# Two 64-byte spacers in an encoder block: the transposed input and the last two 14 KB places move by 64 bytes in SBUF

## The chip, the cores and the metric

The kernel runs on one core of one Trainium2 chip. The metric is device time in microseconds (us) of one execution; lower is better. SBUF addresses below are bytes within a partition, the same in all 128 partitions.

## What is computed

One bidirectional encoder block on x of 512 x 2048, in float32:

```
h = rmsnorm(x); q, k, v of 16 heads = h @ w_in
heads 0-7:  three dilated windows, merged by their softmax denominators   (group A)
heads 8-15: softmax(q1 k1) - lambda * softmax(q2 k2), times v, rmsnorm    (group B)
x = x + concat(heads) @ w_out
h = rmsnorm(x)
x = x + (silu(h @ w_gate) * (h @ w_up)) @ w_down        # inner width 5632
out = rmsnorm(x)
```

## The kernel before, in words

Every large product is made of three matmuls in the float32r type (`mm3`, lines 183 to 186): each operand is split into a high part and the rest, and high x high, high x low and low x high are added up in PSUM. A matmul has a stationary operand, 128 columns loaded into TensorE by a weight load, and a moving operand of 256 or 512 columns streamed through it. The profile names a matmul by its operands, the moving one first: `bank<-xt,hi` streams `xt` against stationary `hi`.

The order on TensorE is the order of the code (a manual schedule); side work of attention (`attend_a`, `attend_b`) is mixed in step by step. The stages, in order of time:

- `unit_v` and `unit_qk` (lines 221 to 293): the values of two heads, then queries and keys of each head, from the transposed input `xt`: 16 tiles of 128 x 1024 (512 high, 512 low), 4 KB per partition each. In `unit_v` `xt` is stationary and the weights `hi`, `lo` move, 256 columns. In `unit_qk` the weights are stationary and `xt` moves, 512 columns; six matmuls follow each other, then a step of attention may stand between.
- `unit_out` (lines 452 to 495): the output projection. The 16 heads' outputs (`mix_tile`, line 500) are stationary: ten in 4 KB tiles `m0` to `m9`, the last six in `w0` and `w1`, two places of 14 KB (7 x 512 floats) that hold three each. The weights `hi`, `lo` move, 512 columns.
- `unit_gu` (lines 649 to 722): gate and up projections, 44 units of 7 products (Strassen-like). In a product 8 operands, `cp0` to `cp5` and then `w0` and `w1`, move against the weights (`hi`, `lo`, or `m6` to `m9`), 3 matmuls of 256 columns each: 24 in a product.
- `unit_first`, `unit_dn`, `unit_last` (lines 768 to 907): the down projection. In `unit_dn` the operands `cp` (and `w0` for pairs 7 and 14) are stationary, the weights move, 256 columns. In `unit_last` the stationary operand lies in a `cp` place; of the eight weight pairs that move, 512 columns, three lie in `hi` and `lo` and five in `cp` places (`last_pair`, line 878).

Where tiles lie. Pools are allocated from both ends of SBUF, left and right. All the large tiles are multiples of 512 bytes long, so every tile of a pool has the same address modulo 128, and so has every slice that a matmul takes. In the built program of the kernel before, the left side (`st`, `hi`, `lo`, then `xt`, and after the heads `m0` to `m9`, `w0`, `w1` in the place of `xt`) lies at 32 modulo 128. The right side (`at`, `cp`, `y`, `wk` and the rest) lies at 96. So of the matmuls of 256 and 512 columns some have both operands at the same place modulo 128, and some have them 64 bytes apart:

| matmuls | stage | columns | moving, stationary before | after |
|---|---|---|---|---|
| `hi,xt` `lo,xt` | unit_v | 256 | 32, 32 | 32, 96 |
| `xt,hi` `xt,lo` | unit_qk | 512 | 32, 32 | 96, 32 |
| `hi,w` `lo,w` | unit_out, 6 of 16 heads | 512 | 32, 32 | 32, 96 |
| `hi,m` `lo,m` | unit_out, the other 10 | 512 | 32, 32 | the same |
| `cp,hi` `cp,lo` `cp,m` | unit_gu, 6 of 8 operands | 256 | 96, 32 | the same |
| `w,hi` `w,lo` `w,m` | unit_gu, 2 of 8 operands | 256 | 32, 32 | 96, 32 |
| `hi,cp` `lo,cp` `m,cp` | unit_dn | 256 | 32, 96 | the same |
| `hi,w` `lo,w` `m,w` | unit_dn, pairs 7 and 14 | 256 | 32, 32 | 32, 96 |
| `hi,cp` `lo,cp` | unit_last, 3 of 8 pairs | 512 | 32, 96 | the same |
| `cp,cp` | unit_last, 5 of 8 pairs | 512 | 96, 96 | the same |

The column "after" is what the change below makes of it.

Of the kernel before, what the change touches and what calls it, by code (L numbers as in the profile page):

```python
# [10 lines left out]
F32 = mybir.dt.float32  # L11
# [6 lines left out]
P = 128  # L18
# [27 lines left out]
def encoder_block(ctx: ExitStack, tc: tile.TileContext, io):  # L46
    nc = tc.nc
    pe, act, dve, pool = nc.tensor, nc.scalar, nc.vector, nc.gpsimd
# [14 lines left out]
    def stage(name, bufs, side="left"):  # L63
        return tc.alloc_tile_pool(name=name, bufs=bufs, side=side, reuse_waits="tile")

    bigx = stage("bigx", KT)
    half = stage("half", 16, "right")
    early = stage("early", 1, "right")
    biga = stage("biga", KT, "right")
    pools = {}  # L70
# [206 lines left out]
    def unit_head(h):  # L277

        qk = unit_qk(h)
        if h % 2 == 0 and h < 2 * H - 2:  # L280
            values_of[0] = unit_v(h // 2 + 1)
        for i in range(KT):
            next(qk)
            yield
            if h < 2 * H - 2 and i % 8 == 7:
                for _ in range(4):
                    next(values_of[0])
                    yield
        for _ in qk:
            pass  # L290
        if h % 2 and h < 2 * H - 2:
            for _ in values_of[0]:
                pass
# [158 lines left out]
    def unit_out(c):  # L452
        xr = []
        b = [bank() for _ in range(NT)]
        for kb in range(8):
            wh, wl = batch()
            if c == 3 and kb == 4:
                load_unit(0)
            if c == 3 and kb == 7:
                for n in PRODUCTS[:2]:  # L460
                    make(0, n)
            if kb == 6:
                for t in range(NT):
                    piece = w_tile()
                    nc.sync.dma_start(piece, io["x"][t * P:(t + 1) * P, c * 512:(c + 1) * 512])
                    xr.append(piece)
            for k2 in range(2):
                k = kb * 2 + k2
                if c == 0:
                    while k not in done:  # L470
                        advance()
                    m = mix_tile(k)
                    act.copy(m[:, :512], mixes[k])
                    dve.tensor_sub(m[:, 512:], mixes[k], m[:, :512].bitcast(F32))
                    mixes[k] = m
                m = mixes[k]
                ws = slice(k2 * 512, (k2 + 1) * 512)
                for t in range(NT):
                    mm3(b[t], m[:, t * P:(t + 1) * P], m[:, 512 + t * P:512 + (t + 1) * P], wh[:, ws], wl[:, ws],
                        start=k == 0, stop=k == KT - 1)  # L480
                yield
# [15 lines left out]
    def place(i, dt=F32):  # L497
        return pools["mx"].tile([P, 1024], dt, name=f"m{i}")

    def mix_tile(k):  # L500

        if k < 10:
            return place(k, F32R)
        j, i = divmod(k - 10, 3)
        if i == 0:
            mix_tile.last = pools["mx"].tile([P, 7, 512], F32R, name=f"w{j}")
        return mix_tile.last[:, 2 * i:2 * i + 2].rearrange("p a q -> p (a q)")
# [442 lines left out]
    def drive(unit, rate=1):  # L950
        for _ in unit:
            for _ in range(rate):
                advance()
# [32 lines left out]
    for h in range(2 * H):  # L986
        drive(unit_head(h))
    bigx.release()
    pools["mx"] = stage("mx", 1)
    for c in range(4):  # L990
        drive(unit_out(c), 2 if c == 0 else 1)
# [62 lines left out]
def _build(arrays):  # L1054
    import concourse.bacc as bacc

    nc = bacc.Bacc("TRN2", target_bir_lowering=False, num_devices=1, dynamic_dma_scratch_size=1024)
    io = {n: nc.dram_tensor(n, a.shape, mybir.dt.from_np(a.dtype), kind="ExternalInput").ap()
          for n, a in arrays.items()}
    io["out"] = nc.dram_tensor("out", (S, D), F32, kind="ExternalOutput").ap()  # L1060
    with tile.TileContext(nc) as tc:
        encoder_block(tc, io)
    return nc
# [9 lines left out]
```

## Time and profile before

| what | us |
|---|---|
| median of 3 runs | 2227.66 (2226.16 to 2230.18) |
| the profiled execution, its own time | 2229.82 |
| its span, first to last instruction | 2228.0 |
| TensorE busy within the span | 2195.6 (99%) |
| VectorE, ScalarE busy | 1663.9, 999.4 |
| mean granted TensorE clock | 0.992 |

The profile is of one execution. A matmul's duration in it runs from its start to the modelled end of its pipeline, and matmuls overlap: what TensorE takes for one in a stream is the distance from its start to the start of the next (called pitch below), not its duration.

### The profile page before, as it was taken

How to read it: one execution, taken by the hardware profiler on the slowest of the kernel's cores; microseconds unless marked ns; L12 is line 12 of the kernel's file. 1: busy time of each engine (PE TensorE's matmuls, PEld its weight loads, DVE VectorE, ACT ScalarE, POOL GpSimd, SP SyncE). 2: the span in 40 equal slices, each digit the busy share in tenths (PEclk: the TensorE clock that was granted, in tenths of full speed). 3: DMA queues.
4: the chain of work that ended last, by engine and by line, in shares of the span. 5: the costliest groups of instructions: out<-in, count | busy, mean ns of one | idle time of the engine just before them, and what ended most of it. 6: DMA issues, size and time to landing. Idle time of an engine off the chain costs nothing.

```text
span 2228.0 us, 37887 instructions
## 1 busy us (share of the span) xinstructions
PE 2195.6 (99%) x15754; PEld 2067.2 (93%) x15754; DVE 1663.9 (75%) x2373; ACT 999.4 (45%) x1486; POOL 10.4 (0%) x23
## 2 busy tenths in 40 slices
PE   9999999999999999999999999999999999999997
PEld 8888888888888888999999999999999899999995
DVE  5655555676787447888888888888887597888897
ACT  6333333545555344454444544445444443343443
POOL 0000000000000000000000000000000000000000
PEclk9999999999999999999999999999999999999999
DMA  8222222222222552354454444544445736446344
GB/s 301 84 78 76 85 77 76 76 76 68 67 76 91 165 180 85 124 169 147 132 169 147 165 147 134 170 147 159 151 132 164 312 114 245 156 166 236 114 138 138
DMA packets 86908, 308.59 MB, mean 139 GB/s; under 512 B 10032, under 2 KB 11952, under 8 KB 84304
## 3 DMA queue, kind: packets, MB, share of 16 engines
q1 hardware_dynamic: 81696, 267.11, 36.4%
q0 software_dynamic: 2736, 34.87, 3.8%
q10 hardware_dynamic: 2304, 4.20, 0.5%
q8 instruction: 123, 2.02, 0.4%
q14 instruction: 49, 0.40, 0.1%
HBM read 261.31 MB, written 44.83 MB: 137 GB/s over the span
## 4 chain that ended last, share of the span: by engine, by line
PE 92%; DVE 4%; DMA 2%; ACT 1%; issue 1%; SPq 0%; ACTq 0%; DVEq 0%
PE bank L184 30%; PE bank L186 29%; PE bank L185 29%; PE bank L303 1%; DMA acts_kept<-raw 1%; DVE lo L630 1%; PE bank L403 1%; PE bank L404 1%; DMA st<-w 0%; DVE m L630 0%; PE bank L539 0%; PE bank L428 0%; DMA combos<-y 0%; DMA at<-xT 0%; ACT hi L629 0%
## 5 line engine op out<-in xcount | busy, mean ns | idle before, releaser
L629 ACT CAST hi<-m 128x1024 fp32r<-128x1024 f32 (+1 forms) x208 | 215.0, 1038 | 252.9 <-PE bank L185 125.0
L184 PE MATMUL bank<-cp,hi 128*128 128x256 f32 x1116 | 314.1, 281 | 0.0
L185 PE MATMUL bank<-cp,hi 128*128 128x256 f32 x1116 | 312.2, 280 | 0.0
L186 PE MATMUL bank<-cp,lo 128*128 128x256 f32 x1116 | 312.2, 280 | 0.0
L630 DVE TENSOR_TENSOR lo<-m,hi 128x1024 fp32r<-128x1024 f32 (+1 forms) x208 | 249.6, 1201 | 61.8 <-ACT hi L629 61.5
L121 DVE TENSOR_TENSOR lo<-st,hi 128x1024 fp32r<-128x1024 f32 (+1 forms) x136 | 165.1, 1214 | 141.0 <-ACT hi L120 140.2
L120 ACT CAST hi<-st 128x1024 fp32r<-128x1024 f32 (+1 forms) x136 | 141.7, 1042 | 192.8 <-PE bank L185 74.8
L185 PE MATMUL bank<-lo,cp 128*128 128x256 f32 (+1 forms) x738 | 211.4, 286 | 4.2 <-DVE lo L630 2.7
L184 PE MATMUL bank<-hi,cp 128*128 128x256 f32 (+1 forms) x738 | 211.3, 286 | 0.3 <-ACT hi L120 0.3
L184 PEld LDWEIGHTS bank<-cp,hi 128*128 128x128 f32 x1116 | 211.1, 189 | 0.3 <-DVE wk L679 0.2
L186 PE MATMUL bank<-hi,cp 128*128 128x256 f32 (+1 forms) x738 | 211.0, 286 | 0.0
L185 PEld LDWEIGHTS bank<-cp,hi 128*128 128x128 f32 x1116 | 210.6, 189 | 0.0
L186 PEld LDWEIGHTS bank<-cp,lo 128*128 128x128 f32 x1116 | 210.5, 189 | 0.0
L184 PE MATMUL bank<-xt,hi 128*128 128x512 f32 x512 | 206.3, 403 | 0.0
L184 PE MATMUL bank<-cp,m 128*128 128x256 f32 x732 | 205.6, 281 | 0.1
L186 PE MATMUL bank<-cp,m 128*128 128x256 f32 x732 | 204.2, 279 | 0.0
L185 PE MATMUL bank<-cp,m 128*128 128x256 f32 x732 | 204.2, 279 | 0.0
L186 PE MATMUL bank<-xt,lo 128*128 128x512 f32 x512 | 200.4, 391 | 0.0
L185 PE MATMUL bank<-xt,hi 128*128 128x512 f32 x512 | 199.9, 391 | 0.0
L629 ACT CAST m<-m 128x1024 fp32r<-128x1024 f32 (+1 forms) x112 | 116.8, 1043 | 148.6 <-PE bank L185 88.6
L630 DVE TENSOR_TENSOR m<-m,m 128x1024 fp32r<-128x1024 f32 (+1 forms) x112 | 135.3, 1208 | 41.4 <-ACT m L629 41.2
L185 PE MATMUL bank<-lo,xt 128*128 128x256 f32 x512 | 145.1, 283 | 0.6 <-DVE lo L121 0.6
(276 smaller groups left out, 5920.7 us busy)
## 6 DMA issues: line engine op xcount, KB each, us to landing
st<-w SPq DMA_DIRECT2D x199, 512.0 KB, 3.7
m<-w SPq DMA_DIRECT2D x180, 512.0 KB, 4.4
cp<-combos POOLq DMA_DIRECT2D x17, 1792.0 KB, 16.6
combos<-y SPq DMA_DIRECT2D x57, 512.0 KB, 4.4
combos<-y SPq DMA_DIRECT2D x19, 256.0 KB, 5.2
m<-w SPq DMA_DIRECT2D x12, 384.0 KB, 3.2
at<-x SPq DMA_DIRECT2D x8, 512.0 KB, 9.0
wk<-x SPq DMA_DIRECT2D x16, 256.0 KB, 5.3
```

The source lines that it names most:

```text
L120: act.copy(hi[:, s], st[:, s])
L121: dve.tensor_sub(lo[:, s], st[:, s], hi[:, s].bitcast(F32))
L184: pe.matmul(out, lh, rh, start=start, stop=False, **kw)
L185: pe.matmul(out, lh, rl, start=False, stop=False, **kw)
L186: pe.matmul(out, ll, rh, start=False, stop=stop, **kw)
L303: pe.transpose(b[:, j * P:(j + 1) * P], prob[:, j * P:(j + 1) * P], ident)
L403: pe.matmul(b, q[:, qs], kh[:, cs], start=True, stop=False)
L404: pe.matmul(b, q[:, qs], kl[:, cs], start=False, stop=True)
L629: act.copy(hi[:, :n], w[name])
L630: dve.tensor_sub(lo[:, :n], w[name], hi[:, :n].bitcast(F32))
```

## The change

A pool of one tile of 16 floats per partition (64 bytes) is allocated ahead of the pool of `xt`, and released with it; a second such tile is allocated in the pool of `m0` to `w1` ahead of `w0`. Each is set to zero once by VectorE, since a tile has to be written. In the built program `xt` moves from 32 to 96 modulo 128, and `w0` and `w1` too; `m0` to `m9`, `hi`, `lo` and all that lies on the right stay.

```diff
+    gap = stage("gap", 1)
+    dve.memset(gap.tile([P, 16], F32, name="gap"), 0.0)
     bigx = stage("bigx", KT)
...
         j, i = divmod(k - 10, 3)
+        if k == 10:
+            dve.memset(pools["mx"].tile([P, 16], F32, name="gap"), 0.0)
         if i == 0:
             mix_tile.last = pools["mx"].tile([P, 7, 512], F32R, name=f"w{j}")
...
     bigx.release()
+    gap.release()
     pools["mx"] = stage("mx", 1)
```

The order of instructions is that of before on every engine but VectorE, which has two more. One is its first instruction. The other stands where `unit_out` splits the first head output that goes to `w0` (`w_...<-hf`, line 474 before, 477 after), while the last head's attention still runs (`sm`, `dens`). VectorE before, at that place:

```order
L474 TENSOR_TENSOR m_6717<-hf,m_6717 128x512
L405 TENSOR_REDUCE sm_6486<-bank 128x1 x2
L121 TENSOR_TENSOR lo<-st,hi 128x1024
L408 RECIPROCAL sm_6487<-dens 128x1
L474 TENSOR_TENSOR w_6745<-hf,w_6745 128x512
L409 SCALAR_TENSOR_TENSOR sm_6487<-sm_6487,nlam,dens 128x1
```

And after the change:

```order
L477 TENSOR_TENSOR m_6723<-hf,m_6723 128x512
L408 TENSOR_REDUCE sm_6492<-bank 128x1 x2
L124 TENSOR_TENSOR lo<-st,hi 128x1024
L411 RECIPROCAL sm_6493<-dens 128x1
L509 MEMSET gap 128x16
L477 TENSOR_TENSOR w_6753<-hf,w_6753 128x512
L412 SCALAR_TENSOR_TENSOR sm_6493<-sm_6493,nlam,dens 128x1
```

Only the one row is new; the line numbers shift by 3, and no other instruction changes its place.

## The prediction

> **What bounds the kernel now.** I read the page first, then the list of waits, the stages one by one, and then the start times of matmuls within each stage.
>
> ```profile
> PE 2195.6 (99%) x15754; PEld 2067.2 (93%) x15754; DVE 1663.9 (75%) x2373; ACT 999.4 (45%) x1486; POOL 10.4 (0%) x23
> PE 92%; DVE 4%; DMA 2%; ACT 1%; issue 1%; SPq 0%; ACTq 0%; DVEq 0%
> PE bank L184 <- DVE wk L829: 8.5, 3, 2.8
> ```
>
> TensorE is busy for 99% of the span, and 92% of the chain that ended last lies on it. The longest group of its waits is 8.5 us in all. By stage (columns: length, then busy time and count of TensorE, weight load, VectorE, ScalarE, GpSimd; granted clock; DMA share, GB/s):
>
> ```profile
> 0.00:50.00 50.00, 48.07 (x312) 42.62 (x313) 26.53 (x51) 31.64 (x46) 0.20 (x4) 1.00 0.87 325
> 50.00:675.00 625.00, 623.37 (x3670) 548.83 (x3669) 396.73 (x754) 267.67 (x486) 0.00 (x0) 1.00 0.24 76
> 690.00:830.00 140.00, 140.00 (x664) 116.68 (x663) 64.25 (x97) 53.82 (x83) 0.00 (x0) 1.00 0.46 151
> 890.00:1756.00 866.00, 865.89 (x7265) 864.14 (x7264) 719.91 (x866) 417.70 (x562) 3.83 (x7) 1.00 0.46 153
> 1790.00:2118.00 328.00, 319.46 (x2646) 318.94 (x2645) 278.91 (x299) 127.23 (x139) 6.35 (x12) 0.97 0.48 170
> ```
>
> In the heads (50 to 675), the output projection (690 to 830), gate and up (890 to 1756) and most of the down projection TensorE has no gap. No engine, queue or transfer can give time there; only the pitch of the matmuls can, the distance from one start to the next. The change removes no instruction. What it can alter is this pitch, so the prediction is a sum of pitches times counts.
>
> **The pitch, by width and by places.** The trace of before has all four cases. Start times stand first in each row.
>
> 256 columns, both operands at 32 modulo 128 (`unit_v`): from the first of these rows to the second lie 36 gaps.
>
> ```profile
> 304.80 0.28 PE L184 MATMUL bank<-hi,xt 128*128 128x256 f32 x1
> ...
> 309.10 0.40 PE L184 MATMUL bank<-xt,hi 128*128 128x512 f32 x1
> ```
>
> 4.30 us / 36 = 119.4 ns. 256 columns, operands 64 bytes apart (`unit_dn`, 159 gaps):
>
> ```profile
> 1819.77 0.28 PE L184 MATMUL bank<-m,cp 128*128 128x256 f32 x1
> ...
> 1838.50 0.28 PE L184 MATMUL bank<-hi,cp 128*128 128x256 f32 x1
> ```
>
> 18.73 / 159 = 117.8 ns. In gate and up three quarters of the matmuls are 64 bytes apart (`cp`) and a quarter are not (`w`). Over three products, 72 gaps, in the settled rhythm:
>
> ```profile
> 1009.03 0.29 PE L184 MATMUL bank<-w,hi 128*128 128x256 f32 x1
> ...
> 1017.57 0.29 PE L184 MATMUL bank<-w,m 128*128 128x256 f32 x1
> ```
>
> 8.54 / 72 = 118.6 ns, 0.8 ns above the pure stream of `unit_dn`. With 256 columns "64 bytes apart" is the cheaper case.
>
> With 512 columns it is the dearer one. In `unit_last` both kinds follow each other in one loop, 21 gaps of `cp,cp` (same place) and then 18 of `hi,cp` (64 bytes apart):
>
> ```profile
> 2204.54 0.39 PE L184 MATMUL bank<-cp,cp 128*128 128x512 f32 x1
> ...
> 2209.30 0.39 PE L184 MATMUL bank<-hi,cp 128*128 128x512 f32 x1
> ...
> 2213.50 0.39 PE L184 MATMUL bank<-cp,cp 128*128 128x512 f32 x1
> ```
>
> 4.76 / 21 = 226.7 ns against 4.20 / 18 = 233.3 ns. Queries and keys (`unit_qk`, same place before) settle at the former value in a long run (32 gaps), but not right after an interruption (5 gaps):
>
> ```profile
> 311.16 0.39 PE L184 MATMUL bank<-xt,hi 128*128 128x512 f32 x1
> ...
> 318.42 0.39 PE L186 MATMUL bank<-xt,lo 128*128 128x512 f32 x1
> ...
> 328.51 0.40 PE L185 MATMUL bank<-xt,hi 128*128 128x512 f32 x1
> 328.75 0.40 PE L186 MATMUL bank<-xt,lo 128*128 128x512 f32 x1
> ...
> 329.67 0.39 PE L184 MATMUL bank<-at 128*128 128x512 f32 x1
> ```
>
> 7.26 / 32 = 226.9 ns and 1.16 / 5 = 232 ns. Most runs are six long and never settle. Of 1402 gaps from one `unit_qk` matmul to another, 69 are stretched by transposes ahead of them; the other 1333 average 228.8 ns, between the two rows.
>
> **The change part by part.** How many matmuls change their case, one row for each group (lines 185 and 186 have as many again):
>
> ```profile
> L184 PE MATMUL bank<-xt,hi 128*128 128x512 f32 x512 | 206.3, 403 | 0.0
> L184 PE MATMUL bank<-hi,xt 128*128 128x256 f32 x512 | 145.3, 284 | 0.0
> L184 PE MATMUL bank<-w,hi 128*128 128x256 f32 x372 | 105.9, 285 | 0.0
> L184 PE MATMUL bank<-w,m 128*128 128x256 f32 x244 | 69.3, 284 | 2.0 <-ACT w L559 2.0
> L184 PE MATMUL bank<-hi,w 128*128 128x512 f32 x96 | 37.6, 392 | 0.0
> L184 PE MATMUL bank<-hi,w 128*128 128x256 f32 x84 | 23.8, 283 | 0.0
> L184 PE MATMUL bank<-m,w 128*128 128x256 f32 x28 | 8.4, 302 | 0.0
> ```
>
> - *Queries and keys* go from the same place to 64 bytes apart: from 228.8 to 233.3 ns on 1333 gaps, 4.5 x 1333 = **+6.0 us**. Bounds: short runs might settle at once at 226.7 (-2.8 us), or stay unsettled and dearer than now: one gap of the short run above is 240 ns, its five average 232, and midway, 236, gives +9.6 us. I take 233.3: it is the only row of that case at this width.
> - *Output projection*, six of sixteen heads: 3 x 96 = 288 matmuls from 226.7 to 233.3, **+1.9 us**. This is `unit_last`'s case exactly, moving at 32 and stationary at 96.
> - *Gate and up*: all 24 matmuls of a product become 64 bytes apart. (372 + 244) x 3 / 6 = 308 products x 24 x 0.8 ns = **-5.9 us**. Bounds: 0, if `w` keeps its pitch, to 10% more.
> - *Values*: 3 x 512 = 1536, of which the first 192 run while TensorE is still fed by DMA (0 to 50 us, share 0.87) and are left out. 1344 x (119.4 - 117.8) = **-2.2 us**; bounds 0 and -2.5.
> - *Down projection, pairs 7 and 14*: 3 x (84 + 28) = 336 x 1.6 to 2 ns = **-0.6 us**.
> - *The two memsets* cost VectorE what this one does:
>
> ```profile
> 1.08 0.06 DVE L961 MEMSET epsc<- 128x1 f32 x1
> 3.07 5.61 DMA at<-xT
> 684.88 0.67 DVE L474 TENSOR_TENSOR w<-hf,w 128x512 fp32r<-128x512 f32 x1
> ```
>
> The first ends some 7 us before the first x lands (second row, from the chain), which holds the first real matmul; had it no such cover, it would cost 0.06 us. The second stands ahead of the split of the first `w0` output (third row), and with it the last head's softmax steps and a weight split queue behind. It writes a place that `xt` held, whose last reader ran at 675 us; the split behind it had to wait for the same reader. TensorE shows no gap from 690 to 830. Nothing, or at worst 0.1 us.
>
> Sum: 6.0 + 1.9 - 5.9 - 2.2 - 0.6 = **-0.8 us**. The profiled execution (2229.82, its span and 1.8 us around it) would come to 2229.0, the median of 2227.66 to 2226.9. The runs of before spread over 4 us, so within 0.2% (4.5 us) a measurement can't tell it from no change.
>
> [...]
>
> **The rivals.**
>
> - *Faster: the dear case is one-sided.* In `unit_last` the moving operand lies at 32 and the weights at 96; in `unit_qk` it will be the other way round. If only the former is dear, queries and keys stay at 228.8: -0.8 - 6.0 = -6.8, about 2220.8, and if they settle at 226.7 too, 2218.0. For it: no long 512-column run of that side is in the trace. Against: with 256 columns both sides cost the same, `cp` at 96 over `hi` in gate and up and `hi` at 32 over `cp` in the down projection, so the places seem to count modulo 128, where the two sides are one.
> - *Slower: what gate and up pay is not the distance.* If `w0` and `w1` are dear because the stream changes place at all after `cp5`, the -5.9 stays out: +5.1, about 2232.8. It decides from 5.3 us of the 5.9 on (-0.8 + 5.3 = 4.5). For it: the excess shows only around the six matmuls of a product that switch. Against: 119.4 ns in `unit_v`, which switches nothing, is the same sort of excess.
> [...]
>
> **How the numbers follow.** Forecast 0.62, faster rival 0.20, slower rival 0.10, no effect 0.08. The forecast's own range, with the bounds of queries and keys (-8.8 to +3.6 about the term, the low end unlikely) and 2 us of scatter, is 2222 to 2231.5. The faster rival ends at 2220.8, so 2220.0 to 2231.5 leaves out the far part of it and the slower rival, under 2 in 10. Faster by over 0.2% (below 2223.2): most of the faster rival and a little of the forecast, 0.23. Slower (above 2232.1): 0.11. Within: 0.66.
>
> **What would show it.** In the changed profile: `unit_qk` gaps near 233 ns in long runs, where 226.9 stood; three products of gate and up in 8.48 us instead of 8.54; `hi,xt` near 117.8 ns; `hi,w` of the output projection near 233. The heads should take some 4 us longer, gate and up 6 us less. The forecast is wrong if long runs of `xt,hi` stay at 227 ns, or if a product of gate and up still takes 2.847 us.

## The result and the profile after

| | us |
|---|---|
| before, median (4 runs) | 2227.85 (2226.16 to 2230.18) |
| after, median (4 runs) | 2213.2 (2210.45 to 2214.96) |
| ratio, 95% interval | 0.9945 (0.9924 to 0.9965) |

Faster by 0.55%, where no change was forecast, and below the stated range. Measured a second time, the same kernel had a ratio of 0.9947 (0.9934 to 0.9959), with medians of 2213.55 (5 runs) and 2223.97 (9 runs).

The page of the changed kernel, its first line and the busy times:

```profile
span 2210.8 us, 37889 instructions
...
PE 2176.4 (98%) x15754; PEld 2044.8 (92%) x15754; DVE 1660.9 (75%) x2375; ACT 1000.3 (45%) x1486; POOL 10.4 (0%) x23
```

TensorE is still what the kernel waits for, with as many instructions and 19 us less busy time. Where the time went is read from the start of each stage's first matmul: output projection, gate and up, `unit_first`, `unit_last`. Before:

```profile
666.19 0.50 PE L184 MATMUL bank<-hi,m 128*128 128x512 f32 x1 [1.46 <-ACT m L473]
861.53 0.28 PE L184 MATMUL bank<-cp,m 128*128 128x256 f32 x1
1747.54 0.40 PE L184 MATMUL bank<-hi,m 128*128 128x512 f32 x1
2166.83 0.39 PE L184 MATMUL bank<-cp,cp 128*128 128x512 f32 x1
```

After:

```profile
660.70 0.50 PE L187 MATMUL bank<-hi,m 128*128 128x512 f32 x1 [1.46 <-ACT m L476]
857.92 0.28 PE L187 MATMUL bank<-cp,m 128*128 128x256 f32 x1
1739.79 0.40 PE L187 MATMUL bank<-hi,m 128*128 128x512 f32 x1
2149.08 0.40 PE L187 MATMUL bank<-cp,cp 128*128 128x512 f32 x1
```

The differences of neighbouring rows are the stages' lengths. The same was read from a second profile of either kernel (`again_before`, `again_after`, below):

| stage | before | after | difference | second pair |
|---|---|---|---|---|
| heads, with the load of x | 666.2 | 660.7 | -5.5 | -5.5 |
| output projection | 195.3 | 197.2 | +1.9 | +1.9 |
| gate and up | 886.0 | 881.9 | -4.1 | -4.5 |
| down projection up to `unit_last` | 419.3 | 409.3 | -10.0 | -2.3 |
| `unit_last` to the end | 61.2 | 61.7 | +0.5 | -0.2 |

Three stages repeat to 0.4 us in these two pairs. (In three later profiles with the input at the new place the heads took 661.7, 664.6 and 662.4 us, the second of them with 6.8 us at half clock while x was loaded; with the input at the old place, 667.3 in `w_only`.) The down projection doesn't repeat; that needs its own explanation. The pitches after, in the runs that answer to those of before. Values (30 gaps), then queries and keys right behind them (42 gaps):

```profile
302.31 0.28 PE L187 MATMUL bank<-hi,xt 128*128 128x256 f32 x1
...
305.71 0.39 PE L187 MATMUL bank<-xt,hi 128*128 128x512 f32 x1
...
315.33 0.40 PE L187 MATMUL bank<-at 128*128 128x512 f32 x1
```

3.40 / 30 = 113.3 ns where 117.8 was expected, and 9.62 / 42 = 229.0 where 233.3 was. The values hold 113.3 ns for part of the time: counted in groups of three matmuls, 53% of them ran below 114.7 ns, and most of the others near 117.8. Gate and up over three products (72 gaps), the output projection from `w0` and `w1` (24 gaps), the down projection (600 gaps):

```profile
806.20 0.39 PE L189 MATMUL bank<-hi,w 128*128 128x512 f32 x1
...
811.79 0.39 PE L189 MATMUL bank<-hi,w 128*128 128x512 f32 x1
...
1010.25 0.28 PE L187 MATMUL bank<-w,m 128*128 128x256 f32 x1
...
1018.73 0.28 PE L187 MATMUL bank<-w,hi 128*128 128x256 f32 x1
...
1780.78 0.28 PE L188 MATMUL bank<-lo,cp 128*128 128x256 f32 x1
...
1843.57 0.28 PE L187 MATMUL bank<-m,w 128*128 128x256 f32 x1
...
1848.78 0.28 PE L188 MATMUL bank<-lo,cp 128*128 128x256 f32 x1
```

The output projection runs at 5.59 / 24 = 233 ns and gate and up at 8.48 / 72 = 117.8, both as forecast. The down projection runs at 68.00 / 600 = 113.3 ns, and so do the 554 matmuls up to 1843.57 us (62.79 us), the first one on `w0`: operands that the change did not move at all.

### The profile page after: what moved, and what is told of

Same layout as the page of the kernel before. It is cut to its first block, busy times and chain, and to the rows that moved or that the text cites. A ratio compares the mean times of both kernels' runs of the same rounds, so it can differ in the third digit from the quotient of the medians.

```text
span 2210.8 us, 37889 instructions
## 1 busy us (share of the span) xinstructions
PE 2176.4 (98%) x15754; PEld 2044.8 (92%) x15754; DVE 1660.9 (75%) x2375; ACT 1000.3 (45%) x1486; POOL 10.4 (0%) x23
## 5 line engine op out<-in xcount | busy, mean ns | idle before, releaser
L188 PEld LDWEIGHTS bank<-lo,cp 128*128 128x128 f32 x738 | 139.3, 189 | 6.1 <-DVE lo L124 2.6
```

The costliest lines, as they stand in the source:

```text
L188: pe.matmul(out, lh, rl, start=False, stop=False, **kw)
```

## The experiments

What had to be explained: a pitch of 113.3 ns, which the profile of before hardly shows (4 of 1030 groups of three matmuls in its down projection ran below 114.7 ns, none of 443 in its values), 229 ns where 233.3 was expected, and a stage that gained without being changed. The theories, as they stood from run to run:

- **A**: the down projection reaches 113.3 ns because no same-place stretch of `w0` interrupts it any more; **B**: that gain is chance.
- **C**: places count modulo 128, and which operand lies at 32; **D**: what counts is the difference, moving minus stationary operand, modulo 256. In these terms the change sets values to -64, queries and keys to +64, the output projection's `w` to -64 and gate and up's `w` to +64; `cp` in gate and up was +64 and in the down projection -64 all along.
- **E**: at -64 a stream of 256 columns has two settled pitches, 113.3 and 117.8 ns, and how it starts decides between them.

**Each spacer alone.** `x_only` leaves out the second spacer, `w_only` the first:

```diff
-        if k == 10:
-            dve.memset(pools["mx"].tile([P, 16], F32, name="gap"), 0.0)
```

> Only the spacer at the transposed input; w0 and w1 lie at 32 modulo 128 as before. Theory A (the gain has two sources: values, 256 columns, settle at 113.3 ns instead of 120; the down projection settles at 113.3 instead of 117.8 because no same-place stretch of w interrupts it): heads as with the full change, 5.5 us faster than before, gate and up and down projection as before: about 2222. Rival B (the down projection's gain is chance of entry or of the throttle and has nothing to do with w0 and w1): 113.3 ns stretches may appear in the down projection here too, total 2213 to 2222.

> Only the spacer at w0 and w1; the transposed input lies at 32 modulo 128 as before. Theory A: heads as before (values 120 ns settled, queries and keys 226.7), output projection 1.8 us slower, gate and up 4 us faster, down projection with 113.3 ns stretches and 4 to 9 us faster: 2217 to 2221. Rival B: no 113.3 ns stretches in the down projection unless entry happens to fall so: about 2225.

`x_only` has a ratio of 0.9985 (0.9972 to 0.9998; medians 2220.74 and 2223.11), `w_only` 0.9956 (0.994 to 0.9973; 2214.45). Their stages add up to the change's: the heads were 661.7 us with the input's spacer alone and 667.3 without it, gate and up 885.1 without the other spacer and 879.2 with it. In `x_only` the down projection did show 113.3 ns stretches, which A had not expected and B had allowed, and took 412.7 us; in `w_only` 409.0. Of that difference 2.7 us is time lost at half clock (4.1 and 1.4 us, counted as in the point on the down projection below). `w_only`'s median lies under both forecasts, 2217 to 2221 and about 2225. So A alone does not hold, and B, which says chance, is not refuted by these two runs.

**Other distances.** `gap192` makes both spacers 192 bytes long (48 floats, as here), `gap128` 128 bytes (32 floats):

```diff
-    dve.memset(gap.tile([P, 16], F32, name="gap"), 0.0)
+    dve.memset(gap.tile([P, 48], F32, name="gap"), 0.0)
...
-            dve.memset(pools["mx"].tile([P, 16], F32, name="gap"), 0.0)
+            dve.memset(pools["mx"].tile([P, 48], F32, name="gap"), 0.0)
```

> Both spacers of 192 bytes instead of 64: 64 bytes apart modulo 128 as in the change, but the other side modulo 256 (the input 64 below the weights instead of 64 above). Theory C (only the place modulo 128 counts, and which operand lies at 32): as the change, values 113.3, queries and keys 229, output projection's w 233.3. Theory D (the difference modulo 256 counts): sides swap, values 117.8, queries and keys 233.3 (5 us slower than the change in the heads), output projection's w 229.

> Both spacers of 128 bytes: same place modulo 128, 128 bytes apart modulo 256. Theory C: pitches as before (values 120, queries and keys 226.7 settled, w in gate and up about 120), about 2228. Theory D: pitches that neither kernel shows.

`gap192`: queries and keys (42 gaps), values (30 gaps), output projection's `w` (24 gaps):

```profile
311.56 0.40 PE L187 MATMUL bank<-xt,hi 128*128 128x512 f32 x1
...
321.36 0.39 PE L187 MATMUL bank<-at 128*128 128x512 f32 x1
...
348.98 0.28 PE L189 MATMUL bank<-hi,xt 128*128 128x256 f32 x1
...
352.51 0.28 PE L189 MATMUL bank<-hi,xt 128*128 128x256 f32 x1
...
815.37 0.39 PE L189 MATMUL bank<-hi,w 128*128 128x512 f32 x1
...
820.86 0.39 PE L189 MATMUL bank<-hi,w 128*128 128x512 f32 x1
```

9.80 / 42 = 233.3, 3.53 / 30 = 117.7 and 5.49 / 24 = 228.8 ns: each case has taken the pitch of the other side. The heads took 670.8 us instead of 660.7: queries and keys 5.1 us more, as expected, and the values 4.4 us more on top. C falls, D holds for these pitches. In `gap128` the same run of queries and keys had a pitch of 232.0 ns:

```profile
310.98 0.39 PE L187 MATMUL bank<-xt,hi 128*128 128x512 f32 x1
...
320.72 0.40 PE L187 MATMUL bank<-at 128*128 128x512 f32 x1
```

Same place modulo 128 would have been 226.9, so in this kernel the place modulo 128 does not settle the pitch. The two kernels had one run each, 2213.73 and 2215.99, beside 2223.11. `gap192` is no slower than the change in spite of its heads: `w` in gate and up now lies at -64, where it ran faster (six matmuls of 24, at 114.6 ns on average in 150 products and 117.3 in 147), and the stage took 875.2 us instead of 881.9.

**The same kernels again.**

> The kernel before, unchanged, in a second profile. Theory A (w0 and w1 at the same place keep the down projection out of 113.3 ns): its down projection shows 117.8 and 120 ns alone, as in the first profile. Theory E (two settled pitches, 113.3 and 117.8, are open to every stream whose moving operand lies 64 below the stationary one modulo 256; which one a stretch takes hangs on how it starts, and changes from execution to execution): stretches of 113.3 ns in some part of the down projection, and a time some us below 2227.7.

> The changed kernel, unchanged, against the kernel before with more runs. Theory A: ratio 0.9935 to 0.995 again. Theory E: heads 5 to 5.5 us and gate and up 4 us faster for sure, output projection 1.8 slower, the down projection's part differs from run to run: 7 to 10 us faster, ratio 0.9955 to 0.997.

The second profile of the kernel before, unchanged, at 2223.1 us, has in its down projection (560 gaps):

```profile
1785.68 0.28 PE L184 MATMUL bank<-hi,cp 128*128 128x256 f32 x1
...
1849.14 0.28 PE L186 MATMUL bank<-hi,cp 128*128 128x256 f32 x1
```

63.46 / 560 = 113.3 ns: the kernel before takes the fast pitch too, and the one profile that the prediction had to go by shows it in 4 of 1030 groups. E had expected this; what decides between the two pitches no run shows. `again_after` is given with the result: its ratio, 0.9947, lies in A's range and misses E's (0.9955 to 0.997), so for the total E counted too little.

Which chunks of the down projection run at it, counted over their start times in every profile (share of groups of three matmuls below 114.7 ns, groups that a stall or half clock stretched beyond 130 ns left out; chunks 1 and 3 hold pairs 7 and 14, whose stationary operand lies in `w0`):

| kernel | `cp`, `w0` in the down projection | chunk 0 | 1 | 2 | 3 | 4 |
|---|---|---|---|---|---|---|
| before | -64, 0 | 0% | 0% | 0% | 2% | 0% |
| again_before | -64, 0 | 92% | 4% | 84% | 1% | 0% |
| x_only | -64, 0 | 92% | 4% | 29% | 2% | 0% |
| after | -64, -64 | 92% | 45% | 54% | 14% | 0% |
| again_after | -64, -64 | 92% | 14% | 84% | 99% | 46% |
| w_only | -64, -64 | 13% | 54% | 44% | 54% | 96% |
| both_sides (below) | -64, -64 | 0% | 0% | 86% | 100% | 46% |
| gap192 | -64, +64 | 0% | 93% | 100% | 97% | 46% |
| gap128 | -64, 128 | 93% | 70% | 68% | 73% | 71% |
| gu_side (below) | +64, +64 | 0% | 0% | 0% | 0% | 0% |
| other_side (below) | +64, +64 | 0% | 0% | 0% | 0% | 0% |

With `w0` at the same place as the weights, chunks 1 and 3 hold the fast pitch for 4% at most, in three profiles; with `w0` elsewhere and `cp` at -64 they hold it for 14% to 100%, in eleven cases of twelve. So A fits these two chunks, though its forecast for the kernel before was wrong, and E fits the rest. `w0` need not lie at -64 for that. In `gap192` it lies at +64, and the stream keeps its pitch over it (420 gaps, 90 of them `w0`'s):

```profile
1890.03 0.28 PE L187 MATMUL bank<-hi,w 128*128 128x256 f32 x1
...
1937.63 0.28 PE L187 MATMUL bank<-m,cp 128*128 128x256 f32 x1
```

47.60 / 420 = 113.3 ns. Here 90 matmuls at +64 among 330 at -64 ran at the fast pitch too; the streams that lay at +64 throughout showed it in no group (0% in gate and up of the change, in the down projection of `gu_side`, and in both stages of `other_side`).

**Turning the sides.** If D and E hold, gate and up, whose 7392 matmuls are all at +64 after the change, can be opened to 113.3 ns as well. `gu_side` puts all `cp` another 128 bytes off, with `w0` and `w1` to match:

```diff
+        pools["gr"] = stage("gr", 1, "right")
+        dve.memset(pools["gr"].tile([P, 32], F32, name="gap"), 0.0)
         pools["xa"] = stage("xa", 1, "right")
...
-            dve.memset(pools["mx"].tile([P, 16], F32, name="gap"), 0.0)
+            dve.memset(pools["mx"].tile([P, 48], F32, name="gap"), 0.0)
```

> The changed kernel with cp0 to cp5, w0 and w1 another 128 bytes off, at 96 modulo 256: in gate and up the moving operand then lies 64 below the weights, in the down projection 64 above. Theory D with E (the difference modulo 256 sets which pitches are open): gate and up in part or wholly at 113.3 ns, up to 7392 x 4.5 ns = 33 us faster than the change; the down projection without any 113.3 ns stretch, 3 to 8 us slower. Theory C (modulo 128 alone): as the change, 2213 to 2221.

Ratio 0.9903 (0.9888 to 0.9918), median 2203.69. Gate and up took 870.9 us (881.9 in the change), the down projection 415.4. Gate and up in `gu_side`, 600 gaps, then a stall that ends on ScalarE, and, later in the stage, 2400 gaps:

```profile
884.35 0.28 PE L189 MATMUL bank<-cp,m 128*128 128x256 f32 x1
...
952.35 0.28 PE L189 MATMUL bank<-cp,m 128*128 128x256 f32 x1
...
957.50 0.38 PE L187 MATMUL bank<-cp,hi 128*128 128x256 f32 x1 [0.45 <-ACT wk L689]
...
1393.00 0.28 PE L187 MATMUL bank<-cp,hi 128*128 128x256 f32 x1
...
1675.66 0.28 PE L187 MATMUL bank<-cp,hi 128*128 128x256 f32 x1
```

113.3 ns, and later 282.66 / 2400 = 117.8 in the same code. In this profile the stretches lasted to a stall, one every second unit, and the stream came out of it at 113.3 or at 117.8 ns; one stretch ended at a single gap of 135 ns (at 1119.23 us), where the profile shows no wait. Once at 117.8 without stalls, it stayed there for some 2900 matmuls. 46% of gate and up ran at 113.3 ns. The down projection came out as expected, 6.1 us above the change and with no fast stretch.

**All at -64, all at +64.** `both_sides` lengthens the weight tiles by 128 bytes and lets each use take its place in them; `other_side` has `(not far)` for `far` and so swaps the two places:

```diff
+    def part(name, far):
+        n = turns[name]
+        turns[name] += 1
+        t = (wsh if name == "hi" else wsl).tile([P, 1056], F32R, name=name)
+        o = 32 if ((n % 3 == 2) + (name == "lo") + far) % 2 else 0
+        return t[:, o:o + 1024]
...
-        hi = wsh.tile([P, 1024], F32R, name="hi") if j is None else place(6 + j, F32R)
-        lo = wsl.tile([P, 1024], F32R, name="lo") if j is None else place(8 + j, F32R)
+        far = i < NF
+        hi = part("hi", far) if j is None else place(6 + j, F32R, far)
+        lo = part("lo", far) if j is None else place(8 + j, F32R, far)
```

(`place` chooses in the same way in `m6` to `m9`; in the output projection's last three blocks, for `w0` and `w1`, and in `unit_last` the weights are the far ones.)

> The changed kernel with weight tiles longer by 128 bytes, so that each use can choose its place: every float32r matmul of 256 columns outside attention has its moving operand 64 bytes below the stationary one modulo 256; 512 columns: queries and keys, w and the three pairs of the last unit 64 above, the rest at the same place. Theory D with E: gate and up as in gu_side (10 us below the change), the down projection with 113.3 ns stretches as in the change (4 to 8 us below gu_side), output projection's w 229 instead of 233.3 (1.2 us): 2193 to 2201, below both kernels. Theory C (modulo 128 alone): as the change, 2213.

> The same kernel with the two places swapped in the weight tiles: every float32r matmul of 256 columns outside attention has its moving operand 64 above the stationary one modulo 256, queries, keys and w (512 columns) 64 below. Theory D with E: no stretch at 113.3 ns anywhere, 256 columns 117.8 throughout, queries and keys 233: values 3 us, queries and keys 5 us, the down projection 3 to 8 us above the change, 2224 to 2230. Theory C: as both_sides.

| | median us | ratio to before | values | gate and up, us | at 113.3 ns |
|---|---|---|---|---|---|
| both_sides | 2199.78 (5 runs) | 0.9897 (0.9881 to 0.9912) | 116.8 ns | 864.7 | 62% |
| other_side | 2228.62 (12 runs) | 1.0017 (1.0007 to 1.0027) | 118.0 ns | 879.7 | 0% |

The values column is the mean over all gaps below 260 ns. The same instructions on the same tiles, with slices 128 bytes away, differ by 28.8 us, and both medians lie in the ranges that D with E had given. (In the built programs all distances are as said; in `other_side`, besides, half of the output projection's `hi,m` and `lo,m` lie 128 apart, and that stage took 198.9 us against 196.1.) The down projection of `both_sides`, 413.5 us, was only 1.9 below that of `gu_side`, not 4 to 8: its first two chunks took the slow pitch, and it had 17.1 us at half clock against 10.2. `other_side` shows no stretch at 113.3 ns anywhere, and its queries and keys (42 gaps) are back at 233.3:

```profile
311.43 0.39 PE L196 MATMUL bank<-xt,hi 128*128 128x512 f32 x1
...
321.23 0.40 PE L196 MATMUL bank<-at 128*128 128x512 f32 x1
```

`both_sides` is faster than both kernels. In gate and up, 38% of its 7392 matmuls still run at 117.8 instead of 113.3 ns, an estimated 12.6 us (0.38 x 7392 x 4.5 ns). The stage also runs into ScalarE's work now; TensorE's waits (us in all, times, longest) from 875 to 1720 us, against those of the change from 880 to 1735 (before had none there):

```profile
PE bank L196 <- ACT wk L700: 3.9, 9, 0.6
```

```profile
PE bank L187 <- ACT wk L687: 1.1, 2, 0.7
```

## Why the prediction was wrong, point by point

- **What bounds the kernel**: right. What the runs show of the result is in pitches of TensorE's stream, in its stalls, and in time at half clock, which the prediction did not count.
- **Queries and keys, +6.0**: the first step that failed. It took the pitch of `unit_last` (233.3 ns, at -64) for the stage that came to lie at +64, since "the places seem to count modulo 128, where the two sides are one". The change and `gap192` show two sides that modulo 128 are one: 229.0 ns at +64, 233.3 at -64. All `xt,hi` and `xt,lo` gaps together went from 359.3 to 360.3 us, so the term was +1.0. The faster rival was right for this term (the 1333 gaps averaged 229.3 ns after, 228.8 before), but its total, 2218.0 to 2220.8, still lies above the measured 2213.2. The row it was argued against with, the 117.8 ns that both sides share at 256 columns, was one of two pitches of the -64 side.
- **Values, -2.2**: right in sign, and mis-sized for that reason. At -64 about half of them (53% of the groups) run at 113.3 ns, where the profile of before has no group of the values below 114.7. Their sum went from 185.7 to 179.7 us, -6.0. The bound of -2.5 wasn't one: it took the smallest pitch seen for the smallest there is.
- **Output projection, +1.9**: right. The 288 gaps went from 65.6 to 67.4 us, at 233.3 ns.
- **Gate and up, -5.9**: the pitch was right (8.48 us for three products, as the prediction asked for), the stage gained 4.1 to 4.5. The rest came back as stalls, which the prediction put at nothing: behind the stage's first stall and outside half clock, gaps above 135 ns cost 0.6 us in all before and 2.6 after, 1.2 and 1.9 in the second pair. With that the term is -3.9 and -5.2. In the second pair half clock took another 0.7 us more after than before, which makes it -4.5; the stage measured -4.1 and -4.5.
- **Down projection, -0.6**: the second step that failed. The prediction costed the pairs that change and held the others at 117.8. With `w0` at the same place two chunks held the fast pitch for 4% at most, with `w0` elsewhere for 14% to 100% in eleven cases of twelve (the table of chunks), and how much of the rest holds it differed from execution to execution (chunk 0 of the kernel before: 0% and 92%). The -10.0 and -2.3 of the two pairs of profiles hold time at half clock too: by the trace's record of the granted clock (0.50), this stage had 20.5 us at half clock before and 10.2 after in the first pair, 10.2 and 17.1 in the second. Matmuls of 256 columns started 213.3 ns apart there. Counted over these gaps, what they took beyond 117.8 ns each is 7.5 us before and 4.1 after, 4.5 and 6.9 in the second pair; without it the stage gained 6.5 and 4.8 us.
- **The memsets**: nothing, as forecast, though two readings behind it were off. In the profile of before, the first matmul on `xt` starts at 5.1 us, ahead of the landing at 8.7, so the first memset had some 2.5 us of cover (ScalarE first uses x at 3.6), not 7; and the last matmul on `xt` starts at 664.3 us, not at 675.

```profile
0.81 0.07 DVE L68 MEMSET gap<- 128x16 f32 x1 [0.81 <-PEq L1063]
...
679.40 0.07 DVE L509 MEMSET gap<- 128x16 f32 x1
```

- **The sum**: heads, output projection and gate and up come to -7.7 and -8.1 in the two pairs; predicted was -0.2 (6.0 + 1.9 - 5.9 - 2.2). With -6.5 and -4.8 for the down projection that makes -14 and -13, and the interval of the second measurement (0.9934 to 0.9959, or 9 to 15 us) holds both. That the steps above are the ones that failed is shown; how large the down projection's gain is in a given execution is partly luck.
- **No effect (0.08)**: refuted by `both_sides` and `other_side`, the same instructions 28.8 us apart (2199.78 and 2228.62). At 512 columns the pitch went with the difference of the operands' addresses, 226.7, 229.0 and 233.3 ns at 0, +64 and -64; by what means, no run shows.

What stays open: why a stream at -64 showed two settled pitches (113.3 and 117.8 ns), and what in a stall decides which follows. That needed control of the stall's length, which was not tried. It also stays open why `x_only`, whose profile has heads 4.5 us shorter, has a median only 2.4 us below before; its interval, 0.4 to 6.2 us, holds both.

## What to carry to other kernels

When TensorE is the bound and its stream has no gaps, measure the distance between starts, by shape and by the operands' addresses, before counting instructions: here slices moved by 128 bytes made 28.8 us between `both_sides` and `other_side`, 1.3%. Don't take a pitch seen in one profile for its price, and take a second profile before a stage's length is used as a reference: unchanged, the kernel before held 113.3 ns in 0% of its down projection's first chunk in one profile and in 92% in the other. In this kernel float32r matmuls of 256 columns ran fastest with the moving operand 64 bytes below the stationary one modulo 256 (113.3 ns in 62% of gate and up in `both_sides`, none at 64 above in `other_side`), and long runs of 512 columns with both at the same place (226.7 ns); in queries and keys, six matmuls at a time, 0 and +64 came to 228.8 and 229.3 ns. Only 0, 64 either way and 128 were tried, and what this buys has to be measured again in another kernel.

## What was not expected of the hardware

Pitches measured in this kernel, by the difference of the operands' addresses (moving minus stationary, modulo 256); float32r, 128 stationary columns, at full clock. Each is a mean over the gaps (distances between starts) of one stretch:

| columns | difference | ns | run and stage | gaps |
|---|---|---|---|---|
| 256 | 0 | 120.0 | before, values (305.86 to 308.98 us) | 26 |
| 256 | +64 | 117.8 | after, gate and up (1010.25 to 1018.73 us) | 72 |
| 256 | -64 | 113.3 | after, down projection (1780.78 to 1848.78 us) | 600 |
| 256 | -64 | 117.8 | before, down projection (1819.77 to 1838.50 us) | 159 |
| 512 | 0 | 226.7 | before, `unit_last` (2204.54 to 2209.30 us) | 21 |
| 512 | +64 | 229.0 | after, queries and keys (305.71 to 315.33 us) | 42 |
| 512 | -64 | 233.3 | before, `unit_last` (2209.30 to 2213.50 us) | 18 |
| 512 | 128 | 232.0 | `gap128`, queries and keys (310.98 to 320.72 us) | 42 |

At 256 columns -64 had the lowest pitch, at 512 the highest of 0, +64 and -64. The values of +64 and -64 are those of streams that lay there throughout; in `gap192` six matmuls at +64 were carried along at 113.3 ns by a stream at -64. The ends of the range lie 6.7 ns apart at 256 columns and 6.6 at 512; no run shows where these differences come from.

In the profile of before, 28 runs have twenty or more same-place matmuls of 512 columns without a gap above 260 ns. Six of them stood at 226 to 227 ns from their first gap, the other 22 after four to six gaps of 224 to 236 ns. And in one stretch at half clock (granted clock 0.50, from 1868.1 to 1873.6 us of before) `m,cp` (-64) and `m,w` (0) alike started 213.3 ns apart.
